# Issuing the S5 output matmuls of a tile together, in turn over column quarters, and the projections of two pairs in turn over row halves

## The chip, the cores and the metric

The kernel runs on one core of one Trainium2 chip. A core has TensorE for matmuls (PE in the profile; its weight loads are listed apart as PEld), VectorE (DVE), ScalarE (ACT), GpSimd (POOL) and SyncE (SP), which here issues most of the DMAs. Each engine works through its own instruction stream in order and waits for others by semaphores. The metric is the device time of one execution in microseconds; the time before is the median of three runs.

## The reference

One layer of a streaming encoder on 256 tokens plus 16 learned meta tokens, width 2048, all in fp32. A norm and one input projection feed two groups side by side: a gated recurrence with 8 heads (HGRN) and an S5 state-space group. Then come an output projection and a gated MLP with a short convolution. The part that the change touches is S5: 1024 channels in 64 groups of 16, each with 64 complex states.

```python
bu_re = jnp.einsum('blgh,gph->lbgp', ug, bb_re)
bu_im = jnp.einsum('blgh,gph->lbgp', ug, bb_im)
...
_, _, st_re, st_im = lax.associative_scan(_complex_scan_combine, (a_seq_re, a_seq_im, bu_re, bu_im), axis=0)
y = (jnp.einsum('lbgp,ghp->blgh', st_re, c_re.astype(f32))
     - jnp.einsum('lbgp,ghp->blgh', st_im, c_im.astype(f32)))
y = y.reshape(b_sz, seq_len, D_S5) + d_skip.astype(f32) * uf
y = jax.nn.gelu(y)
y = y * jax.nn.sigmoid(y @ w_glu.astype(f32) + b_glu.astype(f32))
```

So each group's input is projected to its 64 complex states, the states are scanned over the tokens, and the states are projected back to the 16 channels.

## The kernel before, in words

All large products are formed as three float32r matmuls: ACT casts a weight tile to its upper part (`whi`, L160), DVE subtracts to get the lower part (`wlo`, L82, a helper's line), and `mm3` (L184 to L186) issues upper x upper, upper x lower and lower x upper. Three buffers of each part are in rotation. The kernel first norms and transposes the input and then works through the chunks `u0 h0 u1 h1 u2 h2 u3 h3 g0 g1 g2 g3`: `u` chunks are the S5 input, `h` chunks the recurrence's heads, `g` chunks its output gate. Then follow the S5 gate (`w_glu`), the output projection and the feed-forward part.

Each `u` chunk gives two S5 tiles `j` of 128 channels, eight in all. A tile is four pairs `q` of groups, each pair with 2 x 64 states on the 128 partitions and 136 token pairs along the free dimension (the state is carried over odd tokens only). For each pair `s5_tile` does this:

- ACT and DVE build the pair's rotation table `W` (`tmp`, `W`).
- Two projection matmuls (L584), real and imaginary, from the pair's input `R` and the weights `bt` into a PSUM tile `bu`; there are two `bu` buffers. The input takes 64 rows of the array, the lower or the upper half as `q` is even or odd.
- DVE multiplies `W` with `bu` (`P`), POOL adds (`m`), DVE scans twice (L593), multiplies again (`P`), and adds into the state `xo`.
- Four output matmuls: two (L601) for the odd tokens and two (L602) for the even ones, from `xo` and the weights `cp` into the tile's PSUM `yps`. They produce 32 output channels, so they use 32 columns of the array, quarter `q`.

One matmul per tile (L571) starts `yps` with the even tokens' own contribution through `k0`. After the four pairs, DVE folds `yps` into `ysb` (L91), and the GELU follows. Elsewhere, `s5_b` has a set of small matmuls (L550, `ktp`) that also use 32 columns each, quarter by quarter with two matmuls in each.

The order of instructions on each engine is set by a scheduler when the program is built. It takes what is ready by priority; projection matmuls of the chunks have lower priority than S5 and the recurrence and fill PE's stream between them. A tile name like `yps<-xo,cp` means that `yps` is written from `xo` and `cp`.

Of the kernel before, what the change touches and what calls it, by code (L numbers as in the profile page):

```python
# [9 lines left out]
F32 = mybir.dt.float32  # L10
# [8 lines left out]
T = SEQ + NM  # L19
# [51 lines left out]
def hymba_kernel(ctx: ExitStack, tc: tile.TileContext, x, meta, lb_logits, norm_mix, w_in, hg_norm,  # L71
# [6 lines left out]
    def fact(dst, src, func=AF.Identity, **kw):  # L78
        act.activation(out=dst, in_=src, func=func, **kw)  # L79
# [10 lines left out]
    def stt(dst, a, s, b, op0, op1, **kw):  # L90
        dve.scalar_tensor_tensor(out=dst, in0=a, scalar=s, in1=b, op0=op0, op1=op1, **kw)  # L91

    class pri:
        """Shift the scheduling priority of what is traced inside (lower runs first)."""
# [54 lines left out]
    def wsplit(raw, eng=(dve, dve), parts=1, dep=None):  # L149
        res = []  # L150
        n = 1024 // parts
        for hf in range(2):
            hi = wsp.tile([128, 1024], F32R, tag="whi", name="whi")
            lo = wsp.tile([128, 1024], F32R, tag="wlo", name="wlo")
            if dep is not None and dep[hf] is not None:
                # the split input goes first
                act.copy(out=hi[:, 0:1], in_=dep[hf])
            for i in range(parts):
                c = slice(i * n, (i + 1) * n)
                act.copy(out=hi[:, c], in_=raw[:, hf, c])  # L160
                tt(lo[:, c], raw[:, hf, c], hi[:, c].bitcast(F32), SUB, eng[max(hf, i)])
            res.append((hi, lo))
        return res
# [6 lines left out]
    def mm3(accs, units, rhs, n0, n1):  # L170
        """accs[m] += W^T x over the K tiles of `units` [(unit, first K tile)], three exact-product passes."""
# [24 lines left out]
    # ================= phase A: mixers =================  # L196
# [19 lines left out]
    # scratch in the place of the HGRN output and gate, which come later  # L216
# [3 lines left out]
    # the input, transposed: kept as the residual  # L220
# [34 lines left out]
    def sqrt_rs(src, n, nm, p=prm):  # L255
        """-2 / sqrt(src / D + EPS), with a Newton step."""
        v, r, y, t = (p.tile([128, 1], F32, name=nm + c) for c in "vryt")
        fact(r[:n], src, AF.Sqrt, scale=1.0 / D, bias=epst[:n])
        ts(v[:n], src, 1.0 / D, MUL, EPS, ADD)
        dve.reciprocal(out=y[:n], in_=r[:n])  # L260
        stt(t[:n], y[:n], v[:n], y[:n], MUL, MUL)
        stt(y[:n], t[:n], -3.0, y[:n], ADD, MUL)
        return y[:n]

    def row_rs(a, n, parts, nm):
        """-2 / rms of the rows of a, squares summed on two engines."""
# [13 lines left out]
    # keep the tensor engine's clock up until the input is there  # L280
# [6 lines left out]
    def spread(r, n, ps):  # L287
        """r, one value a token on the partitions, to all partitions along the tokens."""
        pe.matmul(ps, r.to_broadcast([n, 128]), ident[0:n, 0:n], start=True, stop=True)
# [100 lines left out]
    # powers of the unit rotation e^{i theta}: slots (-sin, cos, sin)  # L390
# [12 lines left out]
    # zero-order hold: z = (ab - 1) / a  # L403
# [53 lines left out]
    # e^{2 i theta b}, b = 0..16  # L457
# [16 lines left out]
    # C z and C z A, transposed into per-pair block-diagonal form (the imaginary parts negated)  # L474
# [43 lines left out]
    # Tokens go in pairs (even, odd): the state is carried over odd tokens only, x' = A^2 x + (A B u_even + B u_odd),  # L518
    # so that y_odd = Re(C z x') and y_even = Re(C z A x) + Re(C z B) u_even.
# [48 lines left out]

    def s5_tile(j, R, bt, kz, cp):
        yps = py.tile([128, 2, TH], F32, tag="y", name="yps")  # L570
        pe.matmul(yps[:, 0], kz, ysb[:, j, 0], start=True, stop=False, skip_group_check=True)  # L571
        for q in range(4):
            P_ = j * 4 + q
            bu = pbu.tile([128, 2, TH], F32, tag="bu", name="bu")
            W = s5w.tile([128, 3, TH], F32, tag="W", name="W", bufs=3)
            tmp = s5w.tile([128, 2, 68], F32, tag="tmp", name="tmp")
            act.copy(out=W[:, :, 0:17], in_=ew[:, P_])
            for lv, n in ((6, 17), (7, 34), (8, 68)):
                fact(tmp[:, :, 0:n], W[:, 0:2, 0:n], AF.Copy, scale=pw[:, lv, 2, P_:P_ + 1])
                stt(W[:, 1:3, n:2 * n], W[:, 1:3, 0:n], pw[:, lv, 1, P_:P_ + 1], tmp[:, :, 0:n], MUL, ADD)  # L580
                fact(W[:, 0, n:2 * n], W[:, 2, n:2 * n], AF.Copy, scale=-1.0)
            h = slice(64 * (q % 2), 64 * (q % 2) + 64)
            for ri in range(2):
                pe.matmul(bu[:, ri], bt[h, 2 * ri + q // 2], R[h, q // 2], start=True, stop=True)  # L584
            wv = W[:, 0:2]
            win = bass.AP(wv.tensor, wv.offset, [list(wv.ap[0]), [TH, 2], [TH, 2], [1, TH]])
            P = s5w.tile([128, 2, 2, TH], F32, tag="P", name="P")
            m = s5w.tile([128, 2, TH], F32, tag="m", name="m")
            tt(P, win, bu.unsqueeze(1).to_broadcast([128, 2, 2, TH]), MUL)
            tt(m, P[:, :, 0], P[:, :, 1], ADD, pool)  # L590
            rb = r2[:, P_:P_ + 1].to_broadcast([128, TH])
            for i in range(2):
                dve.tensor_tensor_scan(out=m[:, i], data0=rb, data1=m[:, i], initial=0.0, op0=MUL, op1=ADD)  # L593
            P = s5w.tile([128, 2, 2, TH], F32, tag="P", name="P")
            tt(P, win, m.unsqueeze(1).to_broadcast([128, 2, 2, TH]), MUL)
            xo = s5w.tile([128, 2, TH], F32, tag="xo", name="xo")
            tt(xo, P[:, :, 0], P[:, :, 1], ADD)
            pr = slice(32 * q, 32 * q + 32)
            for ri in range(2):
                c0, c1 = (cp[:, q, k, ri].rearrange("p g h -> p (g h)") for k in range(2))  # L600
                pe.matmul(yps[pr, 1], c0, xo[:, ri], start=False, stop=(q == 3 and ri == 1), skip_group_check=True)  # L601
                pe.matmul(yps[pr, 0, 1:TH], c1, xo[:, ri, 0:TH - 1], start=False, stop=(q == 3 and ri == 1),  # L602
                          skip_group_check=True)
# [57 lines left out]
    def hg_group(h0, f, k, q, v, vm):  # L661
# [10 lines left out]
        for l, h in enumerate(LEV):  # L672
# [14 lines left out]
            if h >= 32:  # L687
                # few large blocks: only the products within a block are formed
# [14 lines left out]
            # prefix and suffix products over blocks of 2h  # L703
# [193 lines left out]
    # ================= phase B: feed-forward =================  # L897
# [132 lines left out]
```

## Time and profile before

| what | value |
|---|---|
| median of three runs | 1282.75 us (1282.28 to 1284.86) |
| profiled execution, span | 1281.9 us |
| PE busy | 1259.6 us, 98% |
| DVE busy | 877.2 us, 68% |
| ACT busy | 601.6 us, 47% |
| POOL busy | 109.3 us, 9% |
| granted TensorE clock, mean | 0.993 |
| output matmuls L601 and L602 | 64 each, shown as 128 records each |
| projection matmuls L584 | 64, shown as 128 records |

An fp32 matmul stands in the profile as two records, a float32r one as one. Lengths of neighbouring matmuls overlap, because a matmul's record also covers its way through the array; the distance from start to start is what the stream pays. "Busy" of an engine is the union of its records. The time of the profiled execution lies 0.85 us under the median.

### The profile page before, as it was taken

What the parts mean: (1) busy time and instruction counts of PE and PEld (TensorE: products, weight loads), DVE (VectorE), ACT (ScalarE), POOL (GpSimd) and SP (SyncE); (2) the same over time, 40 slices, a digit from 0 to 9 for tenths busy, and PEclk for the clock granted to TensorE, in tenths of its full rate; (3) what the DMA queues carried; (4) which work ended last, traced back from release to release, by engine and by line L of the source; (5) the groups of instructions that cost most, each with busy time, mean ns of one, the idle gap of its engine ahead of it and who ended that gap; (6) DMA issues with size and microseconds to landing.
All of it is one profiled execution on the core that took longest, in us unless ns stands there. A gap on an engine that the chain in (4) does not pass through costs nothing.

```text
span 1281.9 us, 22789 instructions
## 1 busy us (share of the span) xinstructions
PE 1259.6 (98%) x9299; PEld 1176.5 (92%) x9299; DVE 877.2 (68%) x1516; ACT 601.6 (47%) x1042; POOL 109.3 (9%) x165
## 2 busy tenths in 40 slices
PE   7989999999999999999999999999999999999997
PEld 7978888898998999999999999999999988888886
DVE  8989898888866777686656566565665655555554
ACT  5645656555444546443434334343333434444444
POOL 5482222201000000000000000000000000000000
PEclk9989999999999999999999999999999999999999
DMA  8533333333244556555555555555555555555552
GB/s 259 150 102 106 106 101 110 101 109 122 88 154 131 152 181 195 186 177 184 178 196 171 193 182 180 195 171 194 181 182 194 172 198 195 195 197 197 197 192 104
DMA packets 176297, 210.81 MB, mean 164 GB/s; under 512 B 14773, under 2 KB 168880, under 8 KB 170416
## 3 DMA queue, kind: packets, MB, share of 16 engines
q1 hardware_dynamic: 175871, 209.26, 49.4%
q8 instruction: 73, 1.20, 0.4%
q14 instruction: 33, 0.26, 0.1%
q0 software_dynamic: 320, 0.09, 0.0%
HBM read 206.12 MB, written 2.10 MB: 162 GB/s over the span
## 4 chain that ended last, share of the span: by engine, by line
PE 93%; DVE 2%; POOL 2%; issue 1%; DMA 0%; ACT 0%; SPq 0%; DVEq 0%; ACTq 0%; POOLq 0%
PE acc L186 9%; PE acc L185 8%; PE acc L184 8%; PE ua L185 7%; PE ua L184 7%; PE ga L184 7%; PE ua L186 7%; PE ga L186 6%; PE ga L185 6%; PE d L952 6%; PE d L951 6%; PE d L953 6%; PE bu L584 2%; PE lps L696 1%; PE yps L601 1%
## 5 line engine op out<-in xcount | busy, mean ns | idle before, releaser
L82 DVE TENSOR_TENSOR wlo<-raw,whi 128x1024 fp32r<-128x1024 f32 (+1 forms) x376 | 462.1, 1229 | 337.2 <-ACT whi L160 286.2
L160 ACT CAST whi<-raw 128x1024 fp32r<-128x1024 f32 (+1 forms) x382 | 397.8, 1042 | 539.5 <-PE ga L185 158.3
L184 PE MATMUL ga<-fh,whi 128*128 128x258 f32 x704 | 199.1, 283 | 0.5 <-DVE a L82 0.5
L186 PE MATMUL ga<-fh,wlo 128*128 128x258 f32 x704 | 198.5, 282 | 0.0
L185 PE MATMUL ua<-fl,whi 128*128 128x256 f32 x704 | 198.4, 282 | 0.0
L185 PE MATMUL ga<-fl,whi 128*128 128x258 f32 x704 | 198.1, 281 | 0.0
L186 PE MATMUL ua<-fh,wlo 128*128 128x256 f32 x704 | 197.9, 281 | 0.0
L184 PE MATMUL ua<-fh,whi 128*128 128x256 f32 x704 | 197.9, 281 | 0.0
L186 PE MATMUL acc<-xh,wlo 128*128 128x272 f32 (+1 forms) x640 | 188.4, 296 | 4.6 <-DVE wlo L82 4.6
L185 PE MATMUL acc<-xl,whi 128*128 128x272 f32 (+1 forms) x640 | 188.5, 296 | 3.5 <-DVE xl L82 3.5
L184 PE MATMUL acc<-xh,whi 128*128 128x272 f32 (+1 forms) x640 | 187.4, 295 | 0.4 <-ACT PP L79 0.4
L184 PEld LDWEIGHTS ga<-fh,whi 128*128 128x128 f32 x704 | 133.1, 189 | 0.7 <-DVE a L82 0.7
L185 PEld LDWEIGHTS ga<-fl,whi 128*128 128x128 f32 x704 | 133.5, 190 | 0.0
L184 PEld LDWEIGHTS ua<-fh,whi 128*128 128x128 f32 x704 | 133.2, 189 | 0.0
L186 PEld LDWEIGHTS ua<-fh,wlo 128*128 128x128 f32 x704 | 132.9, 189 | 0.0
L185 PEld LDWEIGHTS ua<-fl,whi 128*128 128x128 f32 x704 | 132.8, 189 | 0.0
L186 PEld LDWEIGHTS acc<-xh,wlo 128*128 128x128 f32 x640 | 122.3, 192 | 11.4 <-issue 5.1
L186 PEld LDWEIGHTS ga<-fh,wlo 128*128 128x128 f32 x704 | 132.7, 189 | 0.0
L185 PEld LDWEIGHTS acc<-xl,whi 128*128 128x128 f32 x640 | 122.3, 191 | 8.8 <-DVE xl L82 4.1
L951 PE MATMUL d<-whi,ah 128*128 128x512 f32 x328 | 127.7, 389 | 0.0
L952 PE MATMUL d<-whi,al 128*128 128x512 f32 x328 | 127.6, 389 | 0.0
L184 PEld LDWEIGHTS acc<-xh,whi 128*128 128x128 f32 x640 | 121.9, 191 | 3.8 <-issue 2.1
(381 smaller groups left out, 1923.3 us busy)
## 6 DMA issues: line engine op xcount, KB each, us to landing
raw<-in_w_ffn_gate SPq DMA_DIRECT2D x44, 1024.0 KB, 5.1
raw<-in_w_ffn_up SPq DMA_DIRECT2D x44, 1024.0 KB, 5.1
raw<-in_w_ffn_down SPq DMA_DIRECT2D x44, 1024.0 KB, 4.8
raw<-in_w_in SPq DMA_DIRECT2D x39, 1024.0 KB, 5.2
raw<-in_w_out SPq DMA_DIRECT2D x16, 1024.0 KB, 5.7
raw<-in_w_glu SPq DMA_DIRECT2D x4, 1024.0 KB, 5.1
x<-in_x SPq DMA_DIRECT2D x4, 512.0 KB, 5.7
out<-ob SPq DMA_DIRECT2D x8, 256.0 KB, 2.7
```

What stands on the lines that cost most here:

```text
L82: eng.tensor_tensor(out=dst, in0=a, in1=b, op=op)
L160: act.copy(out=hi[:, c], in_=raw[:, hf, c])
L184: pe.matmul(accs[m], lh, xh[:, n0:n1], start=first, stop=False)
L185: pe.matmul(accs[m], lh, xl[:, n0:n1], start=False, stop=False)
L186: pe.matmul(accs[m], ll, xh[:, n0:n1], start=False, stop=end)
L584: pe.matmul(bu[:, ri], bt[h, 2 * ri + q // 2], R[h, q // 2], start=True, stop=True)
L601: pe.matmul(yps[pr, 1], c0, xo[:, ri], start=False, stop=(q == 3 and ri == 1), skip_group_check=True)
L696: pe.matmul(ps[:, i], lhs[i], qf[:, 64 * i:64 * (i + 1)], start=True, stop=True)
L951: pe.matmul(dps[t][n], ah[:, tk], hi, start=False, stop=False, skip_group_check=True)
L952: pe.matmul(dps[t][n], al[:, tk], hi, start=False, stop=False, skip_group_check=True)
L953: pe.matmul(dps[t][n], ah[:, tk], lo, start=False, stop=end, skip_group_check=True)
```

## The change

The body of a pair up to `xo` becomes a function `s5_scan`. `s5_tile` now takes the pairs two at a time: it allocates two `bu` tiles and issues their four projection matmuls in the order second pair real, first pair real, second pair imaginary, first pair imaginary, fixed by `issue_after` (an order on one engine without a semaphore). The states of all four pairs are kept in a list (`xo` has five buffers instead of two). Only then `yps` is allocated and started, and the sixteen output matmuls follow in turn over the four quarters: real and imaginary for the odd tokens, then the same for the even ones. The number and the sizes of matmuls and of all other instructions stay as they were. What else the diff touches is comments.

```diff
+    def s5_scan(P_, bu):
...
+        xo = s5w.tile([128, 2, TH], F32, tag="xo", name="xo", bufs=5)
+        tt(xo, P[:, :, 0], P[:, :, 1], ADD)
+        return xo
+
     def s5_tile(j, R, bt, kz, cp):
+        xos = []
+        for q0 in (0, 2):
+
+            bus = [pbu.tile([128, 2, TH], F32, tag="bu", name="bu") for _ in range(2)]
+            def project(i, ri):
+                h = slice(64 * i, 64 * i + 64)
+                return pe.matmul(bus[i][:, ri], bt[h, 2 * ri + q0 // 2], R[h, q0 // 2], start=True, stop=True)
+
+            with tc.issue_after(project(1, 0).ins):
+                with tc.issue_after(project(0, 0).ins):
+                    with tc.issue_after(project(1, 1).ins):
+                        project(0, 1)
+            for i in range(2):
+                xos.append(s5_scan(j * 4 + q0 + i, bus[i]))
+
         yps = py.tile([128, 2, TH], F32, tag="y", name="yps")
         pe.matmul(yps[:, 0], kz, ysb[:, j, 0], start=True, stop=False, skip_group_check=True)
-        for q in range(4):
-            P_ = j * 4 + q
-            bu = pbu.tile([128, 2, TH], F32, tag="bu", name="bu")
...
-            h = slice(64 * (q % 2), 64 * (q % 2) + 64)
-            for ri in range(2):
-                pe.matmul(bu[:, ri], bt[h, 2 * ri + q // 2], R[h, q // 2], start=True, stop=True)
...
-            xo = s5w.tile([128, 2, TH], F32, tag="xo", name="xo")
-            tt(xo, P[:, :, 0], P[:, :, 1], ADD)
-            pr = slice(32 * q, 32 * q + 32)
-            for ri in range(2):
-                c0, c1 = (cp[:, q, k, ri].rearrange("p g h -> p (g h)") for k in range(2))
-                pe.matmul(yps[pr, 1], c0, xo[:, ri], start=False, stop=(q == 3 and ri == 1), skip_group_check=True)
-                pe.matmul(yps[pr, 0, 1:TH], c1, xo[:, ri, 0:TH - 1], start=False, stop=(q == 3 and ri == 1),
+        for ri in range(2):
+            for q in (3, 0, 1, 2):
+                c0 = cp[:, q, 0, ri].rearrange("p g h -> p (g h)")
+                pe.matmul(yps[32 * q:32 * q + 32, 1], c0, xos[q][:, ri], start=False, stop=(ri == 1),
+                          skip_group_check=True)
+        for ri in range(2):
+            for q in range(4):
+                c1 = cp[:, q, 1, ri].rearrange("p g h -> p (g h)")
+                pe.matmul(yps[32 * q:32 * q + 32, 0, 1:TH], c1, xos[q][:, ri, 0:TH - 1], start=False, stop=(ri == 1),
                           skip_group_check=True)
```

How this moves PE's stream is seen at the second tile (`cp_589` is that tile's output weights). Before, a pair's projections and another pair's four output matmuls, each with the wait it carries:

```order
L584 MATMUL bu<-R,bt 128x136 [waits DMAHW5_49,DVE_49]
L584 MATMUL bu<-R,bt 128x136
L571 MATMUL yps<-ysb,k_591 128x136 [waits DVE_49]
L601 MATMUL yps<-xo,cp_589 32x136 [waits DVE_49]
L602 MATMUL yps<-xo,cp_589 32x135
```

The L601 and L602 rows come twice, and the other three pairs of the tile have their own four at later places. In the changed kernel the tile's sixteen stand together, between projection matmuls of a chunk and the first projection of the next tile:

```order
L185 MATMUL acc<-xl,whi 128x272
L186 MATMUL acc<-xh,wlo 128x272
L614 MATMUL yps<-xo,cp_589 32x136 [waits DVE_49]
L614 MATMUL yps<-xo,cp_589 32x136 x7
L619 MATMUL yps<-xo,cp_589 32x135 x8
L600 MATMUL bu<-R,bt 128x136 [waits DMAHW6_49,DVE_49]
L184 MATMUL acc<-xh,whi 128x272
```

Only the first of the sixteen waits for DVE. The four projections of two pairs do not stay together in the changed kernel's stream. The first one stands alone and carries a wait for DVE; the other three follow after some dozens of chunk matmuls, with a wait of their own. The rows before and behind such a group of three on PE:

```order
L184 MATMUL acc<-xh,whi 128x272
L600 MATMUL bu<-R,bt 128x136 [waits DMAHW1_49,DVE_49]
L600 MATMUL bu<-R,bt 128x136 x2
L185 MATMUL acc<-xl,whi 128x272
L186 MATMUL acc<-xh,wlo 128x272
```

Fourteen of the sixteen half-tiles have this form, one and then three; in the other two the four stand together. Before, each pair's two stood together.

More of the change, by code (lines that the diff above doesn't have):

```diff
@@ L567, in s5_split @@
         return (R,)
-    def s5_tile(j, R, bt, kz, cp):
+    def s5_scan(P_, bu):
+        W = s5w.tile([128, 3, TH], F32, tag="W", name="W", bufs=3)
+        tmp = s5w.tile([128, 2, 68], F32, tag="tmp", name="tmp")
+        act.copy(out=W[:, :, 0:17], in_=ew[:, P_])
+        for lv, n in ((6, 17), (7, 34), (8, 68)):
+            fact(tmp[:, :, 0:n], W[:, 0:2, 0:n], AF.Copy, scale=pw[:, lv, 2, P_:P_ + 1])
+            stt(W[:, 1:3, n:2 * n], W[:, 1:3, 0:n], pw[:, lv, 1, P_:P_ + 1], tmp[:, :, 0:n], MUL, ADD)
+            fact(W[:, 0, n:2 * n], W[:, 2, n:2 * n], AF.Copy, scale=-1.0)
+        wv = W[:, 0:2]
+        win = bass.AP(wv.tensor, wv.offset, [list(wv.ap[0]), [TH, 2], [TH, 2], [1, TH]])
+        P = s5w.tile([128, 2, 2, TH], F32, tag="P", name="P")
+        m = s5w.tile([128, 2, TH], F32, tag="m", name="m")
+        tt(P, win, bu.unsqueeze(1).to_broadcast([128, 2, 2, TH]), MUL)
+        tt(m, P[:, :, 0], P[:, :, 1], ADD, pool)
+        rb = r2[:, P_:P_ + 1].to_broadcast([128, TH])
+        for i in range(2):
+            dve.tensor_tensor_scan(out=m[:, i], data0=rb, data1=m[:, i], initial=0.0, op0=MUL, op1=ADD)
+        P = s5w.tile([128, 2, 2, TH], F32, tag="P", name="P")
+        tt(P, win, m.unsqueeze(1).to_broadcast([128, 2, 2, TH]), MUL)
+        xo = s5w.tile([128, 2, TH], F32, tag="xo", name="xo", bufs=5)
+        tt(xo, P[:, :, 0], P[:, :, 1], ADD)
+        return xo
@@ new lines, in s5_tile @@
+    def s5_tile(j, R, bt, kz, cp):
+        xos = []
[8 more added lines that the diff above has]
+                        project(0, 1)
+            for i in range(2):
+                xos.append(s5_scan(j * 4 + q0 + i, bus[i]))
@@ L570, in s5_tile @@
         yps = py.tile([128, 2, TH], F32, tag="y", name="yps")
         pe.matmul(yps[:, 0], kz, ysb[:, j, 0], start=True, stop=False, skip_group_check=True)
-        for q in range(4):
-            P_ = j * 4 + q
-            bu = pbu.tile([128, 2, TH], F32, tag="bu", name="bu")
[L575 to L581, printed above, removed]
-            h = slice(64 * (q % 2), 64 * (q % 2) + 64)
-            for ri in range(2):
[L584 to L595, printed above, removed]
-            xo = s5w.tile([128, 2, TH], F32, tag="xo", name="xo")
-            tt(xo, P[:, :, 0], P[:, :, 1], ADD)
-            pr = slice(32 * q, 32 * q + 32)
-            for ri in range(2):
-                c0, c1 = (cp[:, q, k, ri].rearrange("p g h -> p (g h)") for k in range(2))
-                pe.matmul(yps[pr, 1], c0, xo[:, ri], start=False, stop=(q == 3 and ri == 1), skip_group_check=True)
-                pe.matmul(yps[pr, 0, 1:TH], c1, xo[:, ri, 0:TH - 1], start=False, stop=(q == 3 and ri == 1),
```

## The prediction

> **What bounds the kernel now.** I read the per-engine summary first, then a table of stretches, the waits, and last the order of time around single instructions. The summary and the table (columns: stretch, its length, then busy us and instruction count of PE, PE's weight loads, DVE, ACT and POOL, the granted clock, DMA share, GB/s):
>
> ```profile
> PE 1259.6 (98%) x9299; PEld 1176.5 (92%) x9299; DVE 877.2 (68%) x1516; ACT 601.6 (47%) x1042; POOL 109.3 (9%) x165
> ...
> 94.00:345.00 251.00, 251.00 (x1975) 222.63 (x1974) 217.88 (x463) 141.38 (x395) 50.20 (x67) 1.00 0.34 106
> 94.00:339.70 245.70, 245.70 (x1931) 217.56 (x1931) 214.44 (x457) 139.66 (x392) 50.20 (x67) 1.00 0.34 104
> 94.00:120.00 26.00, 26.00 (x213) 23.03 (x213) 25.90 (x58) 14.48 (x42) 8.88 (x13) 1.00 0.31 91
> 240.00:270.00 30.00, 30.00 (x232) 27.81 (x230) 28.41 (x61) 16.06 (x43) 4.51 (x4) 1.00 0.38 118
> 345.00:390.00 45.00, 45.00 (x369) 42.20 (x368) 28.11 (x52) 22.14 (x41) 0.31 (x1) 1.00 0.42 139
> ```
>
> TensorE sets the time. Nearly all S5 matmuls that the change moves lie in 94 to 345 us; there PE is busy without a gap at full clock, and it stays so behind it. So a microsecond less of PE work in that stretch is at first a microsecond less of kernel. But DVE is the second number to read: 217.88 of 251 us, 87%, and 214.44 of 245.7 up to the last scan result. An engine at 87% cannot follow a PE that gets more than 13% shorter. After 345 us DVE is at 28.11 of 45, 62%: what is won by then is kept.
>
> The waits in 94 to 345 (who waited for whom: us, times, longest) say how much of DVE's rest is PE's doing:
>
> ```profile
> ACT whi L160 <- PE acc L185: 45.5, 33, 4.4
> DVE wlo L82 <- ACT whi L160: 18.1, 22, 2.0
> ```
>
> ACT's weight cast waits for PE to give a buffer back, and DVE's half of the split waits for the cast. 18.1 of DVE's 33 idle us hang on PE's pace and shrink with it. And DVE runs ahead of PE, by the last pair's result and the matmul that reads it:
>
> ```profile
> 339.26 0.43 DVE L82 TENSOR_TENSOR xo<-P 128x272 f32<-128x272 f32 x1
> ...
> 344.12 0.42 PE L601 MATMUL yps<-xo,cp 128*32 128x136 f32 x2
> ```
>
> 344.12 - 339.69 = 4.4 us of lead, which a faster PE may use up.
>
> **Output matmuls.** One pair's four, among projection matmuls (start us, length, engine, line, shapes, records; an fp32 matmul is two records):
>
> ```profile
> 119.60 0.29 PE L186 MATMUL acc<-xh,wlo 128*128 128x272 f32 x1
> 119.73 0.28 PE L184 MATMUL acc<-xh,whi 128*128 128x272 f32 x1
> 119.94 0.42 PE L601 MATMUL yps<-xo,cp 128*32 128x136 f32 x2
> 120.19 0.39 PE L602 MATMUL yps<-xo,cp 128*32 128x135 f32 x2
> 120.42 0.40 PE L601 MATMUL yps<-xo,cp 128*32 128x136 f32 x2
> 120.66 0.39 PE L602 MATMUL yps<-xo,cp 128*32 128x135 f32 x2
> 120.98 0.39 PE L185 MATMUL acc<-xl,whi 128*128 128x272 f32 x1
> 121.21 0.29 PE L186 MATMUL acc<-xh,wlo 128*128 128x272 f32 x1
> ```
>
> From 119.73 to 121.21 is 1.48 us, in which two projection matmuls also started, each worth 0.13 (119.60 to 119.73). So the block costs 1.22: 1.04 for the matmuls (119.94 to 120.98) and 0.18 for getting in and out. A tile has four: 4.88. All four matmuls of a block use one column quarter, so they follow each other at 0.24. In the changed kernel 16 stand together, four for each quarter. Whether different quarters run side by side, the kernel before shows in its small matmuls of L550, eight in the code's order quarter by quarter, each quarter two deep:
>
> ```profile
> 161.01 0.35 PE L550 MATMUL ktp<-cp,eb 128*32 128x32 f32 x16
> ...
> 276.24 0.31 PE L550 MATMUL ktp<-cp,eb 128*32 128x32 f32 x4
> ...
> 308.30 0.30 PE L601 MATMUL yps<-xo,cp 128*32 128x136 f32 x1
> 308.31 0.39 PE L732 MATMUL mps<-qm,km 128*16 128x258 f32 x1
> 308.44 0.28 PE L601 MATMUL yps<-xo,cp 128*32 128x136 f32 x1
> 308.54 0.38 PE L732 MATMUL mps<-qm,km 128*16 128x258 f32 x1
> ```
>
> Sixteen records over four quarters took 0.35 us, four records in one quarter 0.31: twelve more records for 0.04. And at 308.3 long streams overlap: an output matmul and a 258-column one in another quarter start 0.01 apart, and each keeps its pace (0.14 and 0.23 to its second record). So I take full overlap: 16 matmuls for the time of four, plus 0.04 for the staggered starts, 1.08 + 0.18 = 1.26 a tile. Saved: 4.88 - 1.26 = 3.62, times 8 tiles 29 us. Bounds: with no overlap only three ways in and out go, 3 x 0.18 x 8 = 4.3; nothing but new waits (below) makes it a loss.
>
> The Trainium skill, "TensorE: Matmul & The Clock Gate", section "Part 3: Packing small matmuls — row/col tiling", says matmuls are strictly first in, first out, while tiles may overlap. By that rule the second record of a matmul, waiting for its own quarter, would hold all behind it. The L550 rows speak against it here, since there too the second records stand ahead of the next quarter; what it would make of the time is the third rival.
>
> **Projections.** Two in one row half against four over both, and three, and one alone:
>
> ```profile
> 116.89 0.73 PE L584 MATMUL bu<-R,bt 64*128 64x136 f32 x4
> 117.55 0.40 PE L184 MATMUL acc<-xh,whi 128*128 128x272 f32 x1
> ...
> 62.98 0.74 PE L584 MATMUL bu<-R,bt 64*128 64x136 f32 x8
> 63.65 0.39 PE L186 MATMUL acc<-xh,wlo 128*128 128x258 f32 x1
> ...
> 286.90 0.73 PE L584 MATMUL bu<-R,bt 64*128 64x136 f32 x6
> 287.56 0.44 PE L691 MATMUL lps<-qh,kt 128*32 128x32 f32 x8
> ...
> 288.35 0.50 PE L584 MATMUL bu<-R,bt 64*128 64x136 f32 x2
> 288.78 0.35 PE L550 MATMUL ktp<-cp,eb 128*32 128x32 f32 x16
> ```
>
> Start to next instruction: 0.66 for two, 0.67 for four, 0.66 for three, 0.43 for one. Row halves do overlap. But the order of the changed kernel mostly does not keep the four together: the first goes alone, other matmuls follow, then three. So two pairs cost 0.43 + 0.66 with two ways in and out, against 2 x 0.66 with two before. 14 of the 16 half-tiles have this form: 14 x 0.23 = 3.2 us. If the lone one hid wholly behind its neighbours it would be 9; if it costs a full block, nothing.
>
> **The sum on PE:** 29 + 3.2 = 32; where blocks before already stood side by side they shared a way in, so I take 31 (bounds 4 and 38).
>
> **What DVE allows.** Its instructions are the same in number and size. It needs 214.4 us from 94 to the last result. PE without its 31 would want that result after 245.7 + 4.4 - 31 = 219: DVE would have to be 98% busy. What it has shown: 25.90 of 26.00 in 94 to 120, 28.41 of 30 (95%) in 240 to 270. Without the 18 us that hang on PE's pace it keeps some 13 us of idle, 214.4 / 227.9 = 94%. I take 95%: 225.7 us, last result at 319.7, the last batch over at about 321.1 where it was 345.16. So **24 us** of the 31 come through; the rest turns into PE waiting for DVE. Bounds: DVE always busy, PE's 31; DVE no better than its 87%, 4.4 us of lead and nothing else.
>
> **Waits that are added.** The batch waits for the fourth pair's result, and projections and weight matmuls stand behind it on PE; the group of three waits until the second pair has read its PSUM buffer, where before each buffer was asked for one by one. The first costs PE nothing while DVE leads, and the lead goes; this is inside the 95%. No DMA is moved, and ACT at 141 of 251 has room.
>
> **Rivals.**
>
> 1. *DVE is the bound and stays near its old pace* (last result at 90% or less). For: in-order DVE alternates with ACT, POOL and PE in every scan. 214.4 / 0.90 = 238.3, gain 345.16 - 333.7 = 11; between 5 and 17 us, about 1271.
>
> 2. *Slower: the exchange over the two projection buffers.* Pair three cannot start on DVE before the group of three is done, that group not before pair two's read, and PE meets it in order. If DVE has no other work there, each of the 16 half-tiles adds a wait on both engines. It beats the gain of 31 from 31/16 = 1.9 us a half-tile; at 2.5 it is 9 us slower, 1291. Against: 1.9 is three times the group's 0.66, and DVE has weight splits to do meanwhile.
>
> 3. *Strict order on PE:* each matmul holds the next until its first record is out of its quarter, about 0.12 + 0.01. A batch is 16 x 0.13 + 0.18 = 2.3, saving 2.6 x 8 = 21, with the projections 24 on PE; DVE then needs only 95%, so perhaps 22 come through: 1261.
>
> 4. *It does not do what it says:* no overlap of four quarters with 136 columns. 4.3 + 3.2 = 7.5: 1275. Against: the rows at 308.3.
>
> **How the numbers follow.** The profiled execution has a span of 1281.9 us; the runs' median is 1282.75, 0.85 above it, which I add. 1281.9 - 24 + 0.85 = **1258.8**, rounded to 1259. Chances: forecast (17 to 32 us won, 1251 to 1266) 0.68; rival 1 0.15; rival 2 0.05; rival 3 0.05; rival 4 0.04; 0.03 for gain and new waits cancelling. Low end: all of PE's 31, 1252. High end: rival 1 at half its range, 1273, which leaves out rival 2, rival 4 and some of rival 1. What a measurement here can tell from no change is 0.2%, 2.6 us. Faster by more: 0.68 + 0.15 + 0.05 + 0.04 = 0.92, less 0.01 for the weak end of rival 1: 0.91; same 0.04; slower 0.05.
>
> **What would show it.** Output matmuls in blocks of 32 records about 1.3 us long (2.3 would be rival 3, 4.4 rival 4). Groups of six projection records at 0.66. The last block near 320 us; PE no longer 100% busy before it, with waits on DVE results, and DVE at 93 to 97% from 94 us on. Waits of DVE on ACT's cast well under 18 us. Everything behind 390 us as long as before, only earlier. Wrong would be: PE idle of over 20 us in the stretch, or DVE still at 87 to 90%.

## The result, and the profile after

The changed kernel takes **1251.37 us** (median of four runs, 1250.04 to 1254.47). The kernel before, timed beside it, took 1282.51 us. The ratio is 0.975, with a 95% interval of 0.9739 to 0.9762, so 31 us were won. The forecast was 1259, with a range from 1252: the time lies 8 us under the forecast and 0.6 us under the low end. The sum on PE was 31 us, and all 31 came through; the 7 us that DVE was to hold back did not stay behind.

The summary line and the table of stretches of the changed kernel (columns as in the prediction):

```profile
PE 1226.9 (98%) x9299; PEld 1151.9 (92%) x9299; DVE 873.7 (70%) x1516; ACT 601.2 (48%) x1042; POOL 117.0 (9%) x165
...
94.00:310.70 216.70, 216.70 (x1932) 197.63 (x1932) 210.23 (x455) 141.18 (x395) 58.09 (x67) 1.00 0.39 119
94.00:345.00 251.00, 251.00 (x2252) 231.06 (x2251) 236.99 (x507) 157.82 (x427) 58.40 (x68) 1.00 0.40 123
345.00:390.00 45.00, 45.00 (x330) 38.73 (x329) 26.74 (x47) 21.16 (x35) 0.00 (x0) 1.00 0.44 141
```

PE's busy time fell by 32.7 us (1259.6 to 1226.9), and the span, now 1250.6, by 31.3. PE is still busy without a gap from 94 to 345 us. The first of these stretches ends with the last scan result: DVE was busy for 210.23 of 216.70 us, **97%**.

One batch of output matmuls in the middle, and the last one:

```profile
147.69 0.29 PE L186 MATMUL acc<-xh,wlo 128*128 128x272 f32 x1
147.91 0.67 PE L614 MATMUL yps<-xo,cp 128*32 128x136 f32 x16
148.40 0.64 PE L619 MATMUL yps<-xo,cp 128*32 128x135 f32 x16
148.97 0.50 PE L600 MATMUL bu<-R,bt 64*128 64x136 f32 x2
...
313.68 0.67 PE L614 MATMUL yps<-xo,cp 128*32 128x136 f32 x16
314.17 0.64 PE L619 MATMUL yps<-xo,cp 128*32 128x135 f32 x16
314.74 0.39 PE L185 MATMUL acc<-xl,whi 128*128 128x258 f32 x1
```

The 32 records take 1.06 us (147.91 to 148.97, 313.68 to 314.74), where one pair's eight took 1.04 before. The last batch is over at 314.74, where the last block ended at 345.16 before. Behind it the kernel is as long as it was: 1250.6 - 314.74 = 935.9 us, before 1281.9 - 345.16 = 936.7.

The projections, alone and three together:

```profile
108.09 0.50 PE L600 MATMUL bu<-R,bt 64*128 64x136 f32 x2
108.52 0.39 PE L186 MATMUL acc<-xh,wlo 128*128 128x272 f32 x1
...
116.58 0.73 PE L600 MATMUL bu<-R,bt 64*128 64x136 f32 x6
117.24 0.39 PE L184 MATMUL acc<-xh,whi 128*128 128x272 f32 x1
```

0.43 and 0.66 us to the next instruction, as taken from the old kernel's rows.

The waits in 94 to 345 us:

```profile
ACT whi L160 <- PE acc L185: 29.5, 27, 4.1
DVE wlo L82 <- ACT whi L160: 6.2, 7, 1.9
```

DVE's wait for the cast fell from 18.1 to 6.2 us. PE waits for nobody in this stretch.

Where the 31 us went on PE can be added up. The table gives, for each line, the distances from every record's start to the start of PE's next record, summed over the run (us; the rest of PE's stream is left out). It has three of the experiments beside the two kernels:

```
                          before   after   outputs only   one quarter   quarter by quarter
output matmuls              33.2     9.0       10.4           31.5            20.6
projections                 20.7    16.7       20.6           16.3            17.1
chunk and weight matmuls   893.8   890.7      891.3          890.8           890.6
profiled span             1281.9  1250.6     1256.3         1272.5          1260.5
```

Outputs 24.2, projections 4.0, and 3.1 in the stream of chunk and weight matmuls (L184 to L186), which is broken into less often: 31.3.

### The profile page after: what moved, and what is told of

Same layout as the page of the kernel before. It is cut to its first block, busy times and chain, and to the rows that moved or that the text cites. A ratio compares the mean times of both kernels' runs of the same rounds, so it can differ in the third digit from the quotient of the medians.

```text
span 1250.6 us, 22795 instructions
## 1 busy us (share of the span) xinstructions
PE 1226.9 (98%) x9299; PEld 1151.9 (92%) x9299; DVE 873.7 (70%) x1516; ACT 601.2 (48%) x1042; POOL 117.0 (9%) x165
## 4 chain that ended last, share of the span: by engine, by line
PE 92%; DVE 3%; POOL 2%; issue 1%; DMA 1%; ACT 0%; SPq 0%; DVEq 0%; ACTq 0%; POOLq 0%
PE acc L186 9%; PE acc L184 8%; PE acc L185 8%; PE ua L185 7%; PE ua L184 7%; PE ga L184 7%; PE ua L186 7%; PE ga L186 7%; PE ga L185 7%; PE d L970 6%; PE d L969 6%; PE d L968 6%; PE lps L713 1%; PE bu L600 1%; DVE xn L91 1%
## 5 line engine op out<-in xcount | busy, mean ns | idle before, releaser
L184 PE MATMUL ga<-fh,whi 128*128 128x258 f32 x704 | 199.0, 283 | 0.5 <-DVE a L82 0.5
L186 PE MATMUL ga<-fh,wlo 128*128 128x258 f32 x704 | 198.5, 282 | 0.0
L186 PE MATMUL ua<-fh,wlo 128*128 128x256 f32 x704 | 197.9, 281 | 0.0
L184 PE MATMUL ua<-fh,whi 128*128 128x256 f32 x704 | 197.9, 281 | 0.0
L186 PE MATMUL acc<-xh,wlo 128*128 128x272 f32 (+1 forms) x640 | 186.7, 294 | 5.0 <-DVE wlo L82 5.0
L184 PE MATMUL acc<-xh,whi 128*128 128x272 f32 (+1 forms) x640 | 186.4, 294 | 0.4 <-ACT PP L79 0.4
L184 PEld LDWEIGHTS ga<-fh,whi 128*128 128x128 f32 x704 | 133.0, 189 | 0.7 <-DVE a L82 0.7
L184 PEld LDWEIGHTS ua<-fh,whi 128*128 128x128 f32 x704 | 133.1, 189 | 0.0
L186 PEld LDWEIGHTS ua<-fh,wlo 128*128 128x128 f32 x704 | 132.9, 189 | 0.0
L186 PEld LDWEIGHTS ga<-fh,wlo 128*128 128x128 f32 x704 | 132.6, 189 | 0.0
L186 PEld LDWEIGHTS acc<-xh,wlo 128*128 128x128 f32 x640 | 121.4, 190 | 9.4 <-DVE wlo L82 5.6
L184 PEld LDWEIGHTS acc<-xh,whi 128*128 128x128 f32 x640 | 121.1, 190 | 4.1 <-issue 2.0
```

Source lines behind the costliest of these rows:

```text
L184: pe.matmul(accs[m], lh, xh[:, n0:n1], start=first, stop=False)
L186: pe.matmul(accs[m], ll, xh[:, n0:n1], start=False, stop=end)
```

## The experiments

Two questions were open: whether the gain is the overlap of the quarters or only the standing together, and what DVE allows: whether it is close behind PE and soon sets the time, or already does, or neither. Each expectation says what its theories are. Each kernel was timed beside the kernel before; ratios are against it.

### The outputs alone

The batch of sixteen is kept, the projections are the old ones:

```diff
-            bus = [pbu.tile([128, 2, TH], F32, tag="bu", name="bu") for _ in range(2)]
...
             for i in range(2):
-                xos.append(s5_scan(j * 4 + q0 + i, bus[i]))
+                bu = pbu.tile([128, 2, TH], F32, tag="bu", name="bu")
+                h = slice(64 * i, 64 * i + 64)
+                for ri in range(2):
+                    pe.matmul(bu[:, ri], bt[h, 2 * ri + q0 // 2], R[h, q0 // 2], start=True, stop=True)
+                xos.append(s5_scan(j * 4 + q0 + i, bu))
```

> Outputs batched in turn over the quarters as in the changed kernel, projections pair by pair as before. If PE's work alone sets the time (theory A): the batches take 1.06 us as in the changed kernel and save 29 us, so 1282.5 - 29 = 1253 to 1254, 2 to 3 us above the changed kernel. If DVE at 97% is what holds the changed kernel (theory B): the 3 us of the projections are hidden there anyway, and this run comes out within 1 us of the changed kernel, 1251.

Measured: 1258.4 us, ratio 0.9796 (0.9778 to 0.9815). That is a gain of 26 us, where theory A had 29 and theory B 31. The table above holds most of the 5.7 us of span between it and the changed kernel: projections 3.9, outputs 1.4. The second is an effect I had not counted. With another order, other matmuls fell into seven of the eight batches; the trace at one of them:

```profile
182.92 0.67 PE L609 MATMUL yps<-xo,cp 128*32 128x136 f32 x16
183.42 0.40 PE L614 MATMUL yps<-xo,cp 128*32 128x135 f32 x4
183.75 1.10 PE L708 MATMUL lps<-qh,kt 128*128 128x64 f32 x8
184.78 0.65 PE L614 MATMUL yps<-xo,cp 128*32 128x135 f32 x12
```

A cut batch pays a second way in and out. In the changed kernel three of the eight are cut. PE stayed busy, so this run says nothing against DVE as a limit, and nothing for it.

### The projections alone

The projections of two pairs go together as in the change; each pair's outputs follow its own scan, as before (an excerpt, against the kernel before):

```diff
...
-            for ri in range(2):
-                pe.matmul(bu[:, ri], bt[h, 2 * ri + q // 2], R[h, q // 2], start=True, stop=True)
+            with tc.issue_after(project(1, 0).ins):
+                with tc.issue_after(project(0, 0).ins):
+                    with tc.issue_after(project(1, 1).ins):
+                        project(0, 1)
...
```

> Projections of two pairs in turn as in the changed kernel, outputs pair by pair as before. Theory A: 14 half-tiles times 0.23 us = 3.2 us faster, 1279. Rival, that the lone first projection costs a full way in and out more: no change, 1282. Theory B says nothing else here, since DVE is far from full: 1279.

Measured: 1281.85 us, ratio 0.9982 (0.9972 to 0.9991), 2.3 us won; the profiled span fell by 3.2 (1281.9 to 1278.7). The size is that of the sum, 3.2, and the exchange over the two buffers, rival 2, costs nothing that can be seen.

### All outputs through one column quarter

Sixteen together, but all in quarter 0. The output of S5 is then not the reference's, since all four pairs are added into one quarter; and the matmul that starts the tile covers both halves (an excerpt):

```diff
-                pe.matmul(yps[32 * q:32 * q + 32, 1], c0, xos[q][:, ri], start=False, stop=(ri == 1),
+                pe.matmul(yps[0:32, 1], c0, xos[q][:, ri], start=False, stop=(ri == 1),
...
```

> The changed kernel with all sixteen output matmuls of a tile written to column quarter 0, so that nothing overlaps; the S5 output is therefore not the reference's. One matmul per tile covers 272 columns instead of 136 (about 0.23 us more each, 1.9 in all). If overlap of the quarters is what gains (A and B): blocks of about 3.7 to 3.8 us, only the ways in and out are saved (4.3) and the projections (3.2), less 1.9: about 1277. If standing together is what gains: within 3 us of the changed kernel, 1251 to 1254.

Measured: 1274.63 us, ratio 0.9931 (0.9917 to 0.9946), 9 us won. A batch that no other matmul falls into now takes 3.81 us:

```profile
303.81 2.04 PE L614 MATMUL yps<-xo,cp 128*32 128x136 f32 x16
305.69 2.00 PE L619 MATMUL yps<-xo,cp 128*32 128x135 f32 x16
307.62 0.39 PE L184 MATMUL acc<-xh,whi 128*128 128x258 f32 x1
```

So the overlap of the quarters is what gains: 3.81 against 1.06 us for the same 32 records, 2.75 x 8 = 22 us, and 1274.63 - 1251.37 = 23 us lie between the two medians. Standing together alone is worth 9 us with the projections, near the 7.5 of rival 4. The longer starting matmuls cost about 1 us of it (all of them together 2.1 us from start to start in the changed kernel, 3.4 here).

### Quarter by quarter

Still sixteen together and in four quarters, but with one quarter's four matmuls behind each other, in the order in which the small matmuls of L550 stand:

```diff
-        for ri in range(2):
-            for q in (3, 0, 1, 2):
-                c0 = cp[:, q, 0, ri].rearrange("p g h -> p (g h)")
...
+        for q in (3, 0, 1, 2):
+            pr = slice(32 * q, 32 * q + 32)
+            for ri in range(2):
+                c0, c1 = (cp[:, q, k, ri].rearrange("p g h -> p (g h)") for k in range(2))
...
```

> The sixteen output matmuls stand together, but quarter by quarter, four in a row in each, instead of in turn. If each quarter has a queue of its own on PE: blocks of 1.06 to 1.2 us as in the changed kernel, same time, 1251 within 1.5. If PE keeps strict order: only the seam between two quarters overlaps, blocks of about 3.6 us, so 8 times 2.5 = 20 us slower than the changed kernel, 1271.

Measured: 1262.55 us, ratio 0.9835 (0.9818 to 0.9851), 21 us won: between the two theories, and neither holds. One batch in the trace:

```profile
149.50 0.42 PE L615 MATMUL yps<-xo,cp 128*32 128x136 f32 x2
149.75 0.39 PE L616 MATMUL yps<-xo,cp 128*32 128x135 f32 x2
149.98 0.42 PE L615 MATMUL yps<-xo,cp 128*32 128x136 f32 x4
150.21 0.42 PE L616 MATMUL yps<-xo,cp 128*32 128x135 f32 x4
...
151.20 0.42 PE L616 MATMUL yps<-xo,cp 128*32 128x135 f32 x4
151.46 0.40 PE L615 MATMUL yps<-xo,cp 128*32 128x136 f32 x2
151.69 0.39 PE L616 MATMUL yps<-xo,cp 128*32 128x135 f32 x2
152.01 0.50 PE L600 MATMUL bu<-R,bt 64*128 64x136 f32 x2
```

Each row is a quarter of a microsecond. The first two rows have two records each and so come from one quarter alone; then come six rows of four records, two from each of two quarters; the last two rows are one quarter alone again. The starts of the single records say how: 0, 140, 255 and 370 ns, and then two close together, 485 and 491 ns: the fifth record of the first quarter and the first of the next. So by these records the next quarter begins when the first has three records left to start, not when it has four. That makes 20 steps of 0.116 us instead of 32 or 8: 20 x 0.116 = 2.3, and with the way out of 0.2 the 2.51 of 149.50 to 152.01. Against the changed kernel it is (2.51 - 1.06) x 8 = 11.6 us; the medians differ by 1262.55 - 1251.37 = 11.2. Taking the quarters in turn is thus a part of the gain, and the L550 rows of the prediction could not show it, because they have only four records to a quarter.

The Trainium skill, "TensorE: Matmul & The Clock Gate", section "Part 3: Packing small matmuls — row/col tiling", has matmuls start and end in strict order. By the strict rule as the prediction worked it out, the next quarter would have to wait for the last record of the one before; these rows differ from it: a quarter in use does hold back what is behind, but only from the fifth record on, and the next quarter's first record starts (491 ns) before three records that stand ahead of it in the program (601, 717 and 832 ns, read as the same quarter's by their lines and pace). The rows decide here.

### More work for DVE, in the changed kernel

The last add of each pair is done twice (the second gives the same result):

```diff
         tt(xo, P[:, :, 0], P[:, :, 1], ADD)
+        tt(xo, P[:, :, 0], P[:, :, 1], ADD)
```

> The changed kernel with the last add of each pair (DVE, 0.456 us) done twice: 32 times 0.456 = 14.6 us more on DVE before the last result, nothing else. The changed kernel's DVE is busy 210.2 of 216.7 us up to that result, so 8 to 9 us of the 14.6 find no room even if every idle moment is used. Theory A (PE sets the time, DVE has its 6 us left): 8 to 9 us slower, 1260. Theory B (DVE at 97% already is the bound): 13 to 15 us slower, 1265. If DVE could hide it all, 1251.

Measured: 1253.76 us, ratio 0.9761 (0.9745 to 0.9777), within the uncertainty of the changed kernel's 0.975; the profiled spans are 1250.2 and 1250.6. DVE's busy time grew by 12.9 us (873.7 to 886.6), and the time shows none of it, against both theories. The stretch up to the last scan result, and the last batch:

```profile
94.00:337.50 243.50, 243.50 (x2160) 223.80 (x2161) 240.56 (x517) 152.46 (x406) 73.72 (x71) 1.00 0.40 123
...
342.01 0.67 PE L615 MATMUL yps<-xo,cp 128*32 128x136 f32 x16
342.50 0.64 PE L620 MATMUL yps<-xo,cp 128*32 128x135 f32 x16
```

DVE was busy for 240.56 of 243.50 us, 98.8%. It was full, and the last batch came 28 us later than in the changed kernel (342.01 against 313.68). PE did not wait all the same: it has all 243.50 us. Other matmuls of the stream stand ahead of S5's there, and that is a matter of the order in which the program was built. Counted in the traces, the last output record of S5 is the 2553rd of PE's 9299 in the kernel before and the 2569th in the changed kernel, but the 2822nd here. The first matmul of the S5 gate, which needs S5's result, stays at the 3016th, 3012th and 3006th.

### The same in the kernel before

```diff
             tt(xo, P[:, :, 0], P[:, :, 1], ADD)
+            tt(xo, P[:, :, 0], P[:, :, 1], ADD)
```

> The kernel before with the same add done twice, 14.6 us more on DVE: 229 of 245.7 us, 93%. If DVE's idle of 31 us in that kernel is only its waiting for PE (what the changed kernel suggests): no change, 1282.5 within 1.5. If about 13 us of that idle are DVE's own, as the prediction took: still room for 14.6 in the rest of 18, but only with the lead of 4.4 us used up, so 0 to 3 us slower.

Measured: 1292.08 us, ratio 1.0058 (1.0043 to 1.0073), **slower by 7.4 us**, more than the 0 to 3 expected. Stretches up to the last scan result and behind it, and then the latter one in the kernel before:

```profile
94.00:365.70 271.70, 271.70 (x2127) 241.88 (x2126) 239.54 (x513) 148.20 (x401) 53.16 (x70) 1.00 0.34 106
390.00:500.00 110.00, 105.98 (x796) 97.45 (x796) 75.56 (x136) 51.97 (x82) 0.00 (x0) 0.98 0.46 145
```

```profile
390.00:500.00 110.00, 109.96 (x861) 103.65 (x861) 81.90 (x148) 55.01 (x87) 0.00 (x0) 1.00 0.52 164
```

Here, too, PE is busy all the way to S5's last result at 365.7, 26 us later than before. The loss comes behind it: between 390 and 500 us PE is busy for 105.98 of 110 us, where it had 109.96 in the kernel before. That is 4 of the 7.4 us; PE's own work grew by another 2.7 (1259.6 to 1262.3). What PE waits for in these 110 us:

```profile
PE acc L184 <- ACT mh L840: 1.6, 1, 1.6
PE acc L186 <- DVE wlo L82: 1.4, 1, 1.4
PE acc L185 <- DVE ml L82: 0.8, 2, 0.6
```

`mh` and `ml` are the input of the output projection, made from the recurrence's result, and not S5's; the last output record of S5 is the 2764th here, well ahead of the S5 gate's first (the 3000th). So the same extra work costs time in the kernel before, with DVE at 88% in this run (239.54 of 271.7), and none that can be measured in the changed kernel, with DVE at 97%. A busy share does not give the distance to the point where it costs. Why the kernel before meets that point at `mh`, and the changed kernel does not, stays open.

### Less work for DVE

The last add of each pair goes to POOL:

```diff
-        tt(xo, P[:, :, 0], P[:, :, 1], ADD)
+        tt(xo, P[:, :, 0], P[:, :, 1], ADD, pool)
```

> The changed kernel with the last add of each pair on POOL instead of DVE: 14.6 us less on DVE (196 of 217, 90%), 41 us more on POOL (1.29 us each, POOL has room), and a state that is ready 0.8 us later. Theory A: no change, 1251 within 1.5. Theory B: faster by 4 to 7 us, 1245.

Measured: 1255.43 us, ratio 0.9774 (0.976 to 0.9789), 2 to 3 us slower than the changed kernel by the ratios (0.975, and 0.9757 timed again below; the intervals still touch), which neither theory has. But this run did not do what it was made for. 32 adds of 0.43 us, 13.8 us, left DVE, and its busy time over the run is still 872.9 us, where it was 873.7. What got longer are other instructions of DVE. Two groups of the stretch from 94 to 345 us, in the changed kernel and here (count, then busy us and mean ns of one):

```profile
L91 DVE SCALAR_TENSOR_TENSOR W<-W,pw,tmp 128x68 f32<-128x68 f32 x30 | 10.9, 365 | 0.0
L82 DVE TENSOR_TENSOR ysb<-ysb,gq 128x258 f32<-128x258 f32 x8 | 3.5, 432 | 0.3 <-ACT gq L79 0.2
```

```profile
L91 DVE SCALAR_TENSOR_TENSOR W<-W,pw,tmp 128x68 f32<-128x68 f32 x30 | 13.2, 440 | 0.0
L82 DVE TENSOR_TENSOR ysb<-ysb,gq 128x258 f32<-128x258 f32 x8 | 4.6, 577 | 0.0
```

What they share is that POOL runs beside them. Of the 30 `W` instructions here, 14 had no POOL instruction running at the same time and took 277 ns in the mean; the other 16 took 583. Of the eight `ysb`, four without took 413 ns and four with took 740. But `P<-W,bu`, which reads one of its two tensors from PSUM, took 709 ns without (9 of 31) and 711 with (22). If each DVE instruction is set against the median of its shape without POOL (over nine of the runs), what POOL adds to their lengths is 21.6 us in the changed kernel and 32.5 here, an estimate; the difference, 10.9, takes back most of the 13.8.

POOL's busy time grew from 117.0 to 143.2 us in exchange, and PE waited 2.3 us in 94 to 345 us (251.00 less 248.68 busy). So the run cannot tell whether DVE's load matters; the last two runs below do that.

### All four projections together

The first projection of two pairs is made to wait until both `bu` buffers are free, so that the four stand together (an excerpt; `last_read` keeps the DVE product that read the last `bu`):

```diff
...
+            first = project(1, 0).ins
+            if last_read[0] is not None:
+                tc.add_manual_dep(first, last_read[0].name, ...)
-            with tc.issue_after(project(1, 0).ins):
+            with tc.issue_after(first):
```

> The changed kernel, but the first projection of two pairs also waits until both buffers are free, so that all four stand together in nearly all half-tiles. PE is relieved of the lone projection and its way in and out, 0.43 + 0.18 = 0.61 us in 14 half-tiles, 8.5 us. PE alone: 1243. DVE alone, which needs 210 us in what would be 208: the gain stops at its last 3%, 2 to 5 us, 1247 to 1249. If waiting for both buffers makes DVE wait in turn: slower than the changed kernel.

Measured: 1251.02 us, ratio 0.9738 (0.9723 to 0.9752). By the records PE has 4.1 us less to do (1222.8 against 1226.9), but, unlike in the changed kernel, it waits in 94 to 345 us:

```profile
PE lps L719 <- DVE S L722: 1.2, 2, 0.7
PE dps L691 <- DVE q L91: 0.7, 1, 0.7
PE acc L186 <- DVE wlo L82: 0.5, 1, 0.5
PE bu L602 <- DMA R<-ysb: 0.4, 1, 0.4
PE lps L719 <- DVE S L82: 0.2, 1, 0.2
```

These are 3.0 us, mostly for the recurrence's results. Since 0.0012 in the ratio is inside the uncertainty, I ran the changed kernel and this one again, side by side on one chip.

> The changed kernel once more, beside the next two on the same chip, since one of them (all four projections together) came out 0.35 us under it on another chip, which says nothing. Expected 1251 us, ratio 0.975.

> All four projections of two pairs together, once more. By the records PE is 4 us less busy than in the changed kernel, but stands 2.6 us longer, waiting for DVE (3.0 us of waits in 94 to 345). If only PE's work counts and waits are added, 1.5 us faster than the changed kernel, ratio 0.9735 to 0.974. If the 0.0012 between the earlier ratios was chance, the same as the changed kernel.

Measured: the change again 1252.34 us (1251.1 to 1253.64), ratio 0.9757 (0.9743 to 0.977); four together 1250.43 (1250.08 to 1250.56), ratio 0.9741 (0.9728 to 0.9754). The runs do not touch, and the difference, 1.9 us, is near the 1.5 expected, though the intervals of the ratios overlap. It is the fastest of the versions that compute the whole, by a hair.

### Four together, with less work for DVE

```diff
-        tt(xo, P[:, :, 0], P[:, :, 1], ADD)
+        tt(xo, P[:, :, 0], P[:, :, 1], ADD, pool)
```

> All four projections together, and the last add of each pair on POOL, which takes some 13 us from DVE. Theory A (in the kernel with four together PE waits because DVE is full): the 3 us of waits go, PE's 4 us are all won, about 1247.5. Theory B (PE waits for the length of the chain through one pair, which the way over POOL makes longer, as in the changed kernel with the add on POOL): waits grow by 2 to 3 us, 1253 to 1254.

Measured: 1254.76 us, ratio 0.9775 (0.9762 to 0.9789), 4.3 us slower than with the add on DVE. PE's waits in 94 to 345 us grew from 3.0 to 7.1 us (251.00 less 243.94 busy), among them

```profile
PE lps L719 <- DVE S L722: 2.4, 5, 1.0
PE yps L620 <- POOL xo L82: 2.3, 2, 1.4
```

This is the sign of theory B, and somewhat more than its size. But as in the other run with POOL, DVE's busy time did not fall (873.0 us, 874.4 without), so the way over POOL costs what these rows show, and theory A was not tested by it.

### Still more work for DVE, in the changed kernel

The last add of each pair is done three times:

```diff
         tt(xo, P[:, :, 0], P[:, :, 1], ADD)
+        tt(xo, P[:, :, 0], P[:, :, 1], ADD)
+        tt(xo, P[:, :, 0], P[:, :, 1], ADD)
```

> The changed kernel with the last add of each pair done three times: twice the extra DVE work of the run with two, some 26 to 29 us in all. With the first half the last block went from 313.7 to 342.3 and the time did not move. Theory A (PE fills the place with other work, but only up to the point where that is used up, which the old kernel with the same extra work passed at 369.6): last block at about 370, and as there PE waits at the change to the next stage, 3 to 8 us, so 1254 to 1259. Theory B (DVE is full from 94 us on, so each us of it counts): 1264 to 1266. Theory C (the place may move without end): 1251.

Measured: 1257.12 us, ratio 0.9794 (0.9781 to 0.9808), 4.8 us slower than the changed kernel beside it. Theory A holds: the last batch begins at 370.45, in three pieces, the last of them 24 records from 371.08, and now PE waits. DVE's busy time is 893.1 us, 19.4 more than in the changed kernel where 26 to 29 were expected. The stretch in which S5 ends, and PE's longest wait from 350 to 400 us:

```profile
345.00:390.00 45.00, 40.23 (x296) 33.98 (x296) 36.08 (x78) 22.90 (x48) 2.88 (x2) 0.92 0.29 95
```

```profile
PE acc L184 <- ACT gh L815: 3.8, 1, 3.8
```

Of the 45 us behind 345, PE has lost 4.8, and 3.8 of them in one wait: the first matmul of the S5 gate needs `gh`, the upper part of S5's result behind its GELU, and there is nothing left in the stream to go ahead of it: S5's last output record is the 3015th on PE here, and the gate's first the 3016th. So in the changed kernel S5 may end 28 us later (342) at no cost that can be measured; 57 us later (371) it costs 4.8.

### Really less work for DVE

The second product of each pair is halved and its add left out, with nothing put on POOL. The state is then one product where it should be the sum of two. Once in the changed kernel, once with all four projections together:

```diff
-        P = s5w.tile([128, 2, 2, TH], F32, tag="P", name="P")
-        tt(P, win, m.unsqueeze(1).to_broadcast([128, 2, 2, TH]), MUL)
         xo = s5w.tile([128, 2, TH], F32, tag="xo", name="xo", bufs=5)
-        tt(xo, P[:, :, 0], P[:, :, 1], ADD)
+        tt(xo, win[:, :, 0], m, MUL)
```

> The changed kernel with the second product of each pair halved and its add left out (the state is then one product instead of the sum of two): 0.71 us of DVE a pair less, 32 pairs, 23 us, and nothing put on POOL. In the run with the add on POOL DVE was as busy as before (872.9 against 873.7 us), so that run did not take anything from it. Theory A (only PE counts, S5 may end late at no cost): the same as the changed kernel, 1251 to 1252, ratio 0.975 to 0.976. Theory B (DVE is close enough behind to cost something): faster, up to 1245.

> The same with all four projections together, where PE waited 3.0 us in 94 to 345 us. Theory A (PE waits there because DVE is full): the waits go, 1247 to 1248. Theory B (the waits come from the order in which results are asked for, whatever DVE's load): waits of about 3 us stay, 1250 to 1251.

Measured, in the changed kernel: 1251.1 us, ratio 0.9741 (0.9726 to 0.9755), the same as the changed kernel's 0.975 and 0.9757 within the uncertainty. The stretch, and DVE's longest wait in it:

```profile
94.00:345.00 251.00, 250.12 (x2246) 229.22 (x2245) 220.86 (x476) 156.66 (x425) 49.46 (x68) 1.00 0.40 123
```

```profile
DVE wlo L82 <- ACT whi L160: 17.6, 19, 2.4
```

DVE is back at 220.86 of 251, 88%, and its wait for the cast at 17.6 us, as in the kernel before (87%, 18.1). What it no longer has to do, it waits. Theory A holds: in the changed kernel DVE's load costs nothing that can be measured (1 to 2 us would lie inside the uncertainty).

With four together: 1247.56 us, ratio 0.971 (0.9694 to 0.9726), where the same without the relief had 0.9738 and 0.9741. PE's waits in 94 to 345 us fell from 3.0 us to

```profile
PE bu L600 <- PE yps L623: 0.4, 1, 0.4
PE lps L712 <- DVE S L720: 0.4, 1, 0.4
PE lps L717 <- DVE S L720: 0.3, 1, 0.3
```

Theory A has the time right, with 1247 to 1248 expected: in that kernel the waits go with DVE's work. Its word "full" is not borne out: DVE was busy there for 240.22 of 251 us, 96%, and with the adds doubled in the changed kernel for 245.50, 98%, where PE waited for nothing. So it is not the share that decides, but whether a result is there when its matmul's turn comes; one step beyond the change, matmuls of the recurrence and of the weight stream began to meet results that were not. The edit also makes the way through one pair 0.71 us shorter, and the program's order is another; these were not separated from the load.

## Why the prediction was wrong in its size

**What bounds the kernel** was right: PE before and after. In all the versions that save PE work the span lies 22 to 30 us above PE's busy time (before 22.3, after 23.6), so PE's work is nearly the whole account.

**Output matmuls and projections** were right. The batch was put at 1.26 with the way in and out; it is 1.06 plus about 0.2. The sum of 29 for the outputs came out as 24.2 in their own time and 3.1 in the stream around them, 27.3; the projections gave 4.0 for 3.2. Together 31.3, predicted 31. That the total fits so closely is partly luck: three of the eight batches are cut, which the sum did not have, and the projections made up for it. The bound "no overlap", 4.3 for the outputs, was about right: with one quarter the outputs' own time fell by 1.7 and the stream's by 3.0, together 4.7. Batches that stay whole would give more, (4.88 - 3.81 - 0.18) x 8 = 7.1, but five of the eight are cut in that run.

**"What DVE allows" is the step that failed**, and the 24 with it: "the rest turns into PE waiting for DVE". The span fell by 31.3 us, and PE did not wait. Two things in it were wrong.

The first is the ceiling of 95%. I took it from 28.41 of 30 us, though the first of the two stretches quoted, 94 to 120 us, had 25.90 of 26.00, and in both PE's pace could hold DVE up. I had worked out that all 31 us would ask 98% of DVE, and set that aside. The changed kernel has DVE at 97.0% up to the last result, with 210.2 us of work instead of the 214.4 that I took, and the run with doubled adds has 98.8%. A share that an engine shows while another holds it up is no ceiling: with 0.71 us a pair taken from it, 23 us in all by the lengths of its instructions (16.8 in its busy time), DVE falls back to 88% at the same time of the kernel. For the changed kernel this is enough: its last output stands nearly where it stood in PE's order (the 2569th record, the 2553rd before), and DVE was there in time.

The second is the step from a late DVE to an idle PE. I fixed the last S5 result at one place in PE's stream and turned every microsecond by which DVE is late there into idle PE. But S5's matmuls go into a stream that has other work ready, and where they stand in it is settled anew when a program is built. With the adds doubled S5's last output is the 2822nd record, 28 us later, and PE has no gap; with the adds tripled it is the 3015th, 57 us later, directly ahead of the S5 gate, and the kernel loses 4.8. In the changed kernel what counts for S5 is this room up to the gate. Had DVE stayed at 95%, S5 would have ended 6 us later than it did (321.1 instead of 314.74), far less than these 28; that it would then have cost nothing was not run.

**The added waits** cost nothing, as the prediction said, though DVE's lead did not go: the last result starts at 310.17 and the last batch at 313.68, where it was 4.4 us of lead before (from the end of the one to the start of the other, now 3.1).

**Rivals.** Rival 1, DVE as a bound at its old pace, does not hold either: DVE went from 87% to 97%. Rival 2, the exchange over the buffers, shows no wait. Rival 3, strict order, is not what the batch in turn does (1.06, not 2.1); an order quarter by quarter would have brought a good part of it. Rival 4 describes the run with one quarter: 1274.6, put at 1275.

**The signs to look for:** blocks of 32 records at about 1.3 with the ways in and out, groups of six at 0.66, the wait on the cast well under 18, the rest of the kernel unchanged: all seen. The last block near 320 and PE no longer 100% busy: neither. DVE at 93 to 97% from 94 us on (236.99 of 251, 94%): seen, but it was no sign of a bound.

**The range** began where all of PE's 31 us come through, so it had no room for the case that did occur, plus what two medians differ by: timed again, the changed kernel took 1252.34 us, 0.3 above the low end.

## What to carry to other kernels

If one engine is busy throughout and its stream is filled from a store of other ready work, a second engine at 97% need not cost anything, as here: ask when its late result is next needed and what the scheduler can put ahead of that, instead of multiplying busy shares. Adding work to the second engine until the time moves measures that room; moving its work to another engine may take nothing from it, as the adds on POOL did. Small matmuls on parts of the array are worth gathering, but the order within the batch counts as much: in turn over the parts 1.06 us, part by part 2.51, all in one part 3.81.

## What the hardware showed that I had not expected

- A quarter of the array that is in use holds back matmuls for other quarters only from a certain depth: with eight records to a quarter, the next quarter's first record started with the fifth (485 and 491 ns into the batch), so never more than two quarters worked at once. With four records to a quarter (L550) all four ran side by side, 16 records in 0.35 us. A depth of three waiting records fits both; no other depth was tried.
- DVE can be kept busy for 98.8% of 243.5 us in a stream that exchanges results with three other engines.
- Instructions of DVE became longer when POOL had more to do: 365 to 440 ns and 432 to 577 ns for two groups of the same shapes, so that moving 13.8 us of adds from DVE to POOL lowered DVE's busy time by 0.8 us. In the run with the adds on POOL, the `W` instructions took 277 ns with no POOL instruction beside them and 583 with one, while `P<-W,bu`, with one input in PSUM, took 709 and 711. The Trainium skill, "GPSIMD Engine Reference", section "1. Specifications", says that GpSimd shares its interfaces to SBUF with VectorE and that the two contend where a VectorE instruction has two SBUF inputs. The trace agrees: the two groups that grew (277 to 583 and 413 to 740 ns beside POOL) read two tensors from SBUF, and the one with a PSUM input stayed at 710. I had not weighed this when I moved the adds.
- The same added instructions on DVE (12.0 and 12.9 us of busy time) cost 7.4 us in the kernel with DVE at 87%, and nothing that can be measured in the one with DVE at 97%.
